# Seven of eight k-tile pairs through Strassen's products, with the first weight sum made by an adding DMA

## The chip, the cores and the metric

The kernel runs on one core of a Trainium2 chip. The metric is the device time of one execution in microseconds (us); the median of several executions counts. The engines are TensorE (PE: matmuls; PEld: its weight loads), VectorE (DVE), ScalarE (ACT), GpSimd (POOL) and SyncE (SP), each with a program order of its own.

## The reference

One encoder layer on 256 positions of width 2048, in float32: a gated feed-forward (FFN) with half weight, a stage of gated mixers, and a second FFN.

```python
def _swiglu(x, w_gate, w_up, w_down):
    return (jax.nn.silu(x @ w_gate) * (x @ w_up)) @ w_down

def _macaron_ffn(x, pre_g, w_gate, w_up, w_down, post_g):
    return x + MACARON_WEIGHT * _rms_norm(_swiglu(_rms_norm(x, pre_g), w_gate, w_up, w_down), post_g)
...
    for l in range(DEPTH):
        h = _macaron_ffn(h, ffn1_pre_g[l], ffn1_w_gate[l], ffn1_w_up[l], ffn1_w_down[l], ffn1_post_g[l])
        h = _gated_mixers(h, mix_pre_g[l], w_in[l], b_gate[l], ...)
        h = _macaron_ffn(h, ffn2_pre_g[l], ffn2_w_gate[l], ffn2_w_up[l], ffn2_w_down[l], ffn2_post_g[l])
```

The hidden width of an FFN is 5632. The change touches the gate and up projections of the two FFNs alone; the mixers (attention, a Fourier branch, projections) stay as they are.

## The kernel before

**Precision.** Every weight piece is split into a high part (a rounded copy that ScalarE makes, `whi`, L104) and a low part (the rest, which VectorE subtracts, `wlo`, L105), and each product is three matmuls (L110 to L112: high by high, low by high, high by low). A tile named `w` holds both parts of a piece in one buffer. A piece is 128 x 1024 (two tiles of 512 columns, "wide" here) or 128 x 512 ("narrow"). So 128 x 1024 of weights cost ScalarE and VectorE one wide operation each, and TensorE 12 matmuls in the plain form.

**Blocks.** An FFN's 5632 hidden columns are 11 blocks of 512. The first two are computed plainly. The other nine of each FFN (18 in all) go through `Line`, a queue of pieces: `feed` adds a piece with what prepares it (its split) and what uses it (its matmuls), and runs the oldest piece's matmuls when eight pieces are waiting (`RING` 6 and `RING_B8` 2). So VectorE and ScalarE work up to eight pieces ahead of TensorE. In these loops the program order on VectorE, ScalarE and TensorE is the order in which the code is written; a piece with `hold` keeps back the preparation of the pieces behind it in the code's order until its use has been written.

One block consists of a **row line** (`row_line`), the down-projection of an earlier block (eight wide pieces, 96 matmuls named `pr`, and eight transposes), and of **eight pairs of k-tiles** of gate and up (`swiglu`, matmuls named `pc`; 16 k-tiles of 128 rows make the depth 2048). At the end of each row column, `out` makes ScalarE copy the sums `pr` into y (`y<-pr`, L696), or into `part`, which GpSimd's adding DMA adds to y (L702).

**Strassen's products.** For a pair of k-tiles the gate and up columns and the two halves of the 256 positions form a 2 x 2 by 2 x 2 block product: plain it takes 8 products (24 matmuls), in Strassen's form 7 (21 matmuls), on prepared sums of the activations (`forms.seven`; the tiles `fh`, `fl`, `frest`) and sums of the weights, which are made for every pair before the split: `minus` (L582, `t<-raw` and `raw<-raw,t`). Here pairs 0, 1, 2, 4, 5, 6 are Strassen's (pieces of 6, 6, 6 and 3 matmuls), pairs 3 and 7 plain (12 and 12). The products p1, p5, p6, p7 gather over the pairs in PSUM banks and are combined once per block, on VectorE, by `add` (L587) between the seventh pair and the end of the plain one: `sums`, `gates`, `ups`. p1, p5, p7 have banks of the pool `ptr`, whose three banks also hold transposes and a few `pr`; p6, g0, g1, u0, u1 have the five of `pmm`.

**Loads.** Weights come by SP's queue (`load`, L85): 512 KB into one of five buffers `raw` (`RAW_BUFS`), and for pairs 0, 2, 4, 6 one load of 1 MB (`raw4`, `RAW_B8`) into a larger buffer of the pool `b8`. A buffer `raw` is free once VectorE has made the low part from it.

Of the kernel before, what the change touches and what calls it, by code (L numbers as in the profile page):

```python
# [45 lines left out]
RAW_B8 = (0, 2, 4, 6)  # L46
# [4 lines left out]
BY_SEVEN = (0, 1, 2, 4, 5, 6)  # L51
# [7 lines left out]
def encoder_layer(  # L59
# [24 lines left out]
    def load(dst, src):  # L84
        nc.sync.dma_start(dst, src)  # L85
# [472 lines left out]
    def swiglu(line, forms, w, hs, behind={}):  # L558
# [22 lines left out]
        def minus(out, a, b):  # L581
            V.tensor_tensor(out=out, in0=a, in1=b, op=ALU.subtract)  # L582

        def add(out, a, b):
            if out not in x:
                x[out] = work(out)
            V.tensor_tensor(out=x[out][:], in0=ps[a][:], in1=x[b][:], op=ALU.add)  # L587
# [5 lines left out]
        def silu(t):  # L593
            g = x["x" + "13"[t]]
            A.activation(g[:], g[:], AF.Silu)

        def times(t):
            g, up = x["x" + "13"[t]], x["x" + "25"[t]]
            V.tensor_tensor(out=up[:], in0=up[:], in1=g[:], op=ALU.mult)
            hs.append(up)  # L600

        def seven(pair, between=None, *then):
            a11, a12, na22, s1, s2, s3, s4 = forms.seven[pair]
            end = pair == BY_SEVEN[-1]
            h = {}

            def first():
                t = chunk.tile([P, WP, NB], F32, tag=("ch_hi", "ch_lo")[BY_SEVEN.index(pair) % 2], name="t13")
                if turn["more"] and pair in RAW_B8:
                    four = big("raw4", F32, [P, 2 * WP, NB])  # L610
                    load(four[:], w[pair // 2].rearrange("p (i k c) -> p i k c", i=2, c=NB)[:, pair % 2])
                    ra, rb = four[:, 0:WP, :], four[:, WP:, :]
                    minus(t[:], four[:, 1:3, :], ra)
                else:
                    ra, rb = raw(pair, 0), raw(pair, 1)
                    minus(t[:, 0, :], ra[:, 1, :], ra[:, 0, :])
# [1 line left out]
                h.update(ra=ra, rb=rb, t=t)
                b = ring(rb[:])
                minus(ra[:, 1, :], rb[:, 0, :], t[:, 0, :])  # L620
                return b

            def second():
                b = ring(h["t"][:])
                minus(h["t"][:, 0, :], h["ra"][:, 1, :], h["rb"][:, 1, :])
                return b

            def two(n, a, m, b, last):
                def use(ws):
                    mul(n, a, ws[0], last)  # L630
                    mul(m, b, ws[1], last)
                return use
# [29 lines left out]
    def row_line(line, ch, w, rb, y, way, ahead):
# [663 lines left out]
def _pairs(g, u):  # L1326
# [57 lines left out]
```

## Time and profile before

| | us |
|---|---|
| time, median of 3 (2003.26 to 2007.38) | 2003.29 |
| profiled execution, its span | 2004.2 |
| TensorE busy | 1984.0 (99%) |
| VectorE busy | 1780.1 (89%) |
| ScalarE busy | 1301.2 (65%) |
| GpSimd busy | 84.5 (4%) |
| one block of the first FFN, from 282.07 to 344.16 | 62.09 |
| its pairs of k-tiles, from 304.73 | 39.43 |

The result lists no own time for the profiled execution beside its span: 2004.2 us is from its first to its last instruction, 0.9 us over the median. A matmul's "busy" is longer than the distance to the next one, since matmuls overlap; the time of a row of matmuls is read from their starts. Two columns in rows of instructions are the start in us from the span's start and the duration; what stands in square brackets is the idle time of the engine ahead of the instruction and what ended it.

### The profile page before, as it was taken

To read this page: it belongs to the slowest core of one execution; us is meant where nothing else is said; L and a number is where in the kernel's file an instruction comes from. 1 tells how busy PE (TensorE), PEld (TensorE's weight loads), DVE (VectorE), ACT (ScalarE), POOL (GpSimd) and SP (SyncE) were. 2 spreads that over 40 slices of the span, in tenths; PEclk is the share of its full clock that TensorE was granted. 3 is DMA by queue.
4 is the path that set the end of the run, shared out by engine and by line. 5 is a ranking of instruction groups with operands and counts; after the bars stand their busy time and mean duration, and the time that the engine had idled before them with its cause. 6 is when DMAs were issued, how large, how long until landed. Compare 5 with 4: busy or idle time off the path is not lost.

```text
span 2004.2 us, 25805 instructions
## 1 busy us (share of the span) xinstructions
PE 1984.0 (99%) x9146; PEld 1644.8 (82%) x9146; DVE 1780.1 (89%) x2352; ACT 1301.2 (65%) x1860; POOL 84.5 (4%) x94
## 2 busy tenths in 40 slices
PE   9999999999999999999999999999999999999998
PEld 7888888888888878888888888878888888888886
DVE  6899999999999878886877885878999999999996
ACT  7566766767667756556666564656677766677666
POOL 0000000000000000100000000000000000000002
PEclk9999999999999999999999999999999999999999
DMA  8657766677668796954555557565577766677673
GB/s 319 211 175 240 225 232 199 200 249 228 226 204 275 250 280 201 261 184 138 195 189 188 192 166 277 194 215 194 169 236 231 231 210 208 213 233 229 208 264 126
DMA packets 117585, 434.20 MB, mean 217 GB/s; under 512 B 12840, under 2 KB 18992, under 8 KB 106064
## 3 DMA queue, kind: packets, MB, share of 16 engines
q1 hardware_dynamic: 103888, 411.65, 59.9%
q0 software_dynamic: 13568, 20.91, 6.0%
q8 instruction: 71, 1.16, 0.2%
q14 instruction: 58, 0.48, 0.1%
HBM read 409.44 MB, written 6.29 MB: 207 GB/s over the span
## 4 chain that ended last, share of the span: by engine, by line
PE 90%; DVE 5%; DMA 3%; ACT 1%; issue 1%; SPq 0%; DVEq 0%; ACTq 0%
PE pc L111 18%; PE pc L112 18%; PE pc L110 18%; PE pr L112 10%; PE pr L111 10%; PE pr L110 10%; DVE wlo L105 2%; PE pt L180 1%; DMA raw<-in_f_gu 1%; DMA raw<-in_w_fo 1%; DVE t L582 0%; PE pe L110 0%; PE pe L112 0%; PE pe L111 0%; PE pt L1072 0%
## 5 line engine op out<-in xcount | busy, mean ns | idle before, releaser
L105 DVE TENSOR_TENSOR wlo<-raw,whi 128x1024 fp32r<-128x1024 f32 (+1 forms) x567 | 681.1, 1219 | 96.9 <-ACT whi L104 95.2
L104 ACT ACTIVATE whi<-raw 128x1024 fp32r<-128x1024 f32 (+1 forms) x567 | 585.8, 1052 | 253.7 <-PE pc L112 109.3
L111 PE MATMUL pc<-wlo,fh 128*128 128x512 f32 x738 | 287.3, 389 | 0.0
L112 PE MATMUL pc<-whi,fl 128*128 128x512 f32 x738 | 287.3, 389 | 0.0
L110 PE MATMUL pc<-whi,fh 128*128 128x512 f32 x738 | 287.1, 389 | 0.0
L110 PE MATMUL pc<-whi,uh 128*128 128x512 f32 x688 | 271.7, 395 | 1.5 <-ACT uh L786 1.5
L111 PE MATMUL pc<-wlo,uh 128*128 128x512 f32 x688 | 269.8, 392 | 1.7 <-DVE wlo L105 1.7
L112 PE MATMUL pc<-whi,ul 128*128 128x512 f32 x688 | 269.6, 392 | 0.0
L104 ACT ACTIVATE whi<-t 128x1024 fp32r<-128x1024 f32 (+1 forms) x198 | 171.6, 867 | 139.4 <-DVE t L582 130.8
L582 DVE TENSOR_TENSOR t<-raw 128x512 f32<-128x512 f32 (+1 forms) x252 | 209.1, 842 | 14.1 <-DMA raw<-in_f_gu 10.3
L110 PE MATMUL pr<-whi,hTh 128*128 128x512 f32 x544 | 213.4, 392 | 0.0
L112 PE MATMUL pr<-whi,hTl 128*128 128x512 f32 x544 | 211.8, 389 | 0.0
L111 PE MATMUL pr<-wlo,hTh 128*128 128x512 f32 x544 | 211.7, 389 | 0.0
L105 DVE TENSOR_TENSOR wlo<-t,whi 128x1024 fp32r<-128x1024 f32 (+1 forms) x198 | 193.6, 978 | 13.4 <-ACT whi L104 13.0
L104 ACT ACTIVATE w<-raw 128x1024 fp32r<-128x1024 f32 x144 | 152.0, 1055 | 40.8 <-DVE raw L582 34.7
L105 DVE TENSOR_TENSOR w<-raw,w 128x1024 fp32r<-128x1024 f32 x144 | 175.6, 1219 | 0.0
L111 PEld LDWEIGHTS pc<-wlo,fh 128*128 128x128 f32 x738 | 138.5, 188 | 29.2 <-DVE wlo L105 0.3
L110 PEld LDWEIGHTS pc<-whi,fh 128*128 128x128 f32 x738 | 138.5, 188 | 28.9
L112 PEld LDWEIGHTS pc<-whi,fl 128*128 128x128 f32 x738 | 138.5, 188 | 28.7
L111 PEld LDWEIGHTS pc<-wlo,uh 128*128 128x128 f32 x688 | 129.8, 189 | 28.5 <-DVE wlo L105 3.6
L110 PEld LDWEIGHTS pc<-whi,uh 128*128 128x128 f32 x688 | 129.7, 188 | 28.5 <-ACT uh L786 2.8
L112 PEld LDWEIGHTS pc<-whi,ul 128*128 128x128 f32 x688 | 129.6, 188 | 27.0
(360 smaller groups left out, 3188.4 us busy)
## 6 DMA issues: line engine op xcount, KB each, us to landing
raw<-in_f_down SPq DMA_DIRECT2D x176, 512.0 KB, 5.0
raw<-in_f_gu SPq DMA_DIRECT2D x144, 512.0 KB, 4.8
raw<-in_f_gu SPq DMA_DIRECT2D x72, 1024.0 KB, 7.0
raw<-in_w_in SPq DMA_DIRECT2D x112, 512.0 KB, 4.5
raw<-in_f_up SPq DMA_DIRECT2D x32, 512.0 KB, 4.5
raw<-in_w_ao SPq DMA_DIRECT2D x32, 512.0 KB, 3.8
raw<-in_w_out SPq DMA_DIRECT2D x32, 512.0 KB, 4.5
raw<-in_f_gate SPq DMA_DIRECT2D x31, 512.0 KB, 5.8
```

The costliest lines, as they stand in the source:

```text
L104: a = A.activation(hi, src, AF.Copy)
L105: v = V.tensor_tensor(out=lo, in0=src, in1=hi.bitcast(F32), op=ALU.subtract)
L110: T.matmul(ps, lh, rh, start=first, stop=False, skip_group_check=onto)
L111: T.matmul(ps, lh, rl, start=False, stop=False, skip_group_check=onto)
L112: return T.matmul(ps, ll, rh, start=False, stop=last, skip_group_check=onto)
L180: T.transpose(pt[:, j, :], src[:, j * P:(j + 1) * P], ident[:])
L582: V.tensor_tensor(out=out, in0=a, in1=b, op=ALU.subtract)
```

## The change

Pair 3 becomes a Strassen pair too; pair 7 alone stays plain. A Strassen pair's weights are combined in another way. The gate columns g0, g1 (512 KB) are loaded into `raw`, the up columns u0, u1 (512 KB) into a tile `ra` in one of six homes that `Sums` hands out (buffers of `b8` and of `chunk`); a DMA on GpSimd's queue adds g0 (256 KB) from memory onto the first half of `ra`. `Sums.get` keeps these loads three pairs ahead (`SUMS_AHEAD`). VectorE then makes one narrow difference `s` (L638) and, once `raw` has been split, one wide difference that overwrites `raw` (L642). The 1 MB loads go. The pieces of a Strassen pair are 6, 6, 3, 6 matmuls. The products are named and combined anew: three combinations instead of four in `sums` (`combine`, L616), and the plain products of u1 are added in the bank of p5 once x4 = p5 - x2 has read it (`onto`), so that the output is x3 - p5. The pool `pmm` then has four names in the block instead of five, and one `pr` moves there from `ptr`. The weights' order in memory for Strassen pairs is the plain one.

```diff
-RAW_B8 = (0, 2, 4, 6)
-BY_SEVEN = (0, 1, 2, 4, 5, 6)
+BY_SEVEN = (0, 1, 2, 3, 4, 5, 6)
+SUMS_AHEAD = 3
...
+    class Sums:
+        def __init__(self, wgu, blocks):
+            self.todo = [(wgu[f], pair) for f in range(blocks) for pair in BY_SEVEN]
+            self.ready, self.n = [], 0
+        def place(self):
+            n = self.n = self.n % 6 + 1
+            if n % 3 == 0:
+                return chunk.tile([P, WP, NB], F32, tag=("ch_hi", "ch_lo")[n // 6], name="ra")
+            if n % 3 == 1:
+                self.two = big("ra2", F32, [P, 2, WP, NB])
+            return self.two[:, n % 3 - 1]
+        def fetch(self):
...
+            ra = self.place()
+            load(ra[:, :, :], src[:, 1])
+            nc.gpsimd.dma_start(ra[:, 0, :], src[:, 0, 0], accum_op=ALU.add)
+            self.ready.append(ra)
+        def get(self):
+            while len(self.ready) <= SUMS_AHEAD and self.todo:
+                self.fetch()
+            return self.ready.pop(0)
...
-                        mul("gu"[i] + str(t), forms.plain[k][t], b[j], k == KD - 1)
+                        n = ("g0", "g1", "u0", "p5")[NT * i + t]
+                        mul(n, forms.plain[k][t], b[j], k == KD - 1, n == "p5")
...
             def first():
-                t = chunk.tile([P, WP, NB], F32, tag=("ch_hi", "ch_lo")[BY_SEVEN.index(pair) % 2], name="t13")
-                if turn["more"] and pair in RAW_B8:
-                    four = big("raw4", F32, [P, 2 * WP, NB])
-                    load(four[:], w[pair // 2].rearrange("p (i k c) -> p i k c", i=2, c=NB)[:, pair % 2])
...
+                h["b"], h["a"], h["s"] = raw(pair, 0), sums_.get(), work("s")
+                V.tensor_tensor(out=h["s"][:], in0=h["a"][:, 0, :], in1=h["a"][:, 1, :], op=ALU.subtract)
+                return ring(h["b"][:])
             def second():
...
+                V.tensor_tensor(out=h["b"][:], in0=h["s"][:].unsqueeze(1).to_broadcast([P, WP, NB]), in1=h["b"][:],
+                                op=ALU.subtract)
+                return ring(h["a"])
...
-            line.feed(first, two("u0", s4, "g0", a12, False))
-            line.feed(second, two("p5", s1, "p7", s3, end), hold=end)
-            line.feed(lambda: ring(h["ra"][:]), two("p1", a11, "p6", s2, end), *then[0:2], hold=end)
-            line.feed(lambda: ring(h["t"][:, 0:1, :]), lambda ws: mul("g1", na22, ws[0]), *then[2:], hold=end)
+            line.feed(first, lambda ws: (mul("p1", a11, ws[0], end), mul("g0", a12, ws[1])))
+            line.feed(second, lambda ws: (mul("p5", s1, ws[0], end), mul("u0", s4, ws[1])), *then[0:1], hold=end)
+            line.feed(lambda: ring(h["s"][:].unsqueeze(1)), lambda ws: mul("p6", s2, ws[0], end), *then[1:3], hold=end)
+            line.feed(lambda: ring(h["b"][:]), lambda ws: (mul("p7", s3, ws[0], end), mul("g1", na22, ws[1])), *then[3:],
+                      hold=end)
...
-        sums = [copy, lambda: add("x2", "p6", "x1"), lambda: add("x3", "p7", "x2"), lambda: add("x2", "p5", "x2"),
-                lambda: add("x5", "p5", "x3")]
+        sums = [copy, lambda: combine("x2", "p6", "x1", ALU.add), lambda: combine("x4", "p5", "x2", ALU.subtract),
+                lambda: combine("x3", "p7", "x2", ALU.add)]
...
-        ups = [lambda: add("x2", "u0", "x2"), lambda: times(0), lambda: add("x5", "u1", "x5"), lambda: times(1)]
+        ups = [lambda: combine("x4", "u0", "x4", ALU.add), lambda: times(0),
+               lambda: combine("x3", "p5", "x3", ALU.subtract), lambda: times(1)]
...
-        rooms = {(0, 0): (ptr, "tr"), (1, 0): (ptr, "tr"), (1, 1): (ptr, "tr")} if not first else {}
+        rooms = {(0, 0): (ptr, "tr"), (1, 0): (ptr, "tr")} if not first else {}
```

VectorE in the pairs of a block before, the end of one pair and the whole of the next, with one plain piece (`raw_2299`) in between (`t13` is the tile `t` of the differences, `raw4` a 1 MB load, `hTl` the low part of the transposed hidden values; where a name ends in a number it is one buffer's):

```order
L105 TENSOR_TENSOR wlo_2241<-raw_2183,whi_2240 128x1024
L105 TENSOR_TENSOR wlo_2259<-t13_2182,whi_2258 128x512
L582 TENSOR_TENSOR t13_2270<-raw4_2271 128x1024
L105 TENSOR_TENSOR w2_2274<-raw4_2271,w2_2274 128x1024
L582 TENSOR_TENSOR raw4_2271<-raw4_2271,t13_2270 128x512
L105 TENSOR_TENSOR wlo_2287<-t13_2270,whi_2286 128x1024
L582 TENSOR_TENSOR t13_2270<-raw4_2271 128x512
L105 TENSOR_TENSOR wlo_2302<-raw_2299,whi_2301 128x1024
L105 TENSOR_TENSOR wlo_2310<-raw4_2271,whi_2309 128x1024
```

and in the changed kernel, one pair at the same place and the first row of the next (`ra2` is the home of the sums):

```order
L638 TENSOR_TENSOR s_2318<-ra2_1901 128x512
L105 TENSOR_TENSOR w2_2320<-raw_2314,w2_2320 128x1024
L642 TENSOR_TENSOR raw_2314<-s_2318,raw_2314 128x1024
L105 TENSOR_TENSOR wlo_2333<-ra2_1901,whi_2332 128x1024
L105 TENSOR_TENSOR wlo_2341<-s_2318,whi_2340 128x512
L105 TENSOR_TENSOR wlo_2353<-raw_2314,whi_2352 128x1024
L638 TENSOR_TENSOR s_2367<-ra_2136 128x512
```

The four wide and three narrow operations of a pair became four wide and two narrow, and `raw` is overwritten in the row behind the one that splits it (`w2`).

ScalarE at the end of the row line before, from the last transposed hidden values (`hTh`) on; the two rows `y<-pr` are the copies of the last row column:

```order
L104 ACTIVATE hTh<-pt 128x4x128 x2
L104 ACTIVATE whi<-raw 128x1024
L696 ACTIVATE y_941<-pr 128x512
L696 ACTIVATE y_942<-pr 128x512
L104 ACTIVATE whi<-t_2722 128x512
L104 ACTIVATE w_2814<-raw_2811 128x1024
```

and now:

```order
L104 ACTIVATE hTh<-pt 128x4x128 x2
L104 ACTIVATE w_2834<-s 128x512
L706 ACTIVATE y_950<-pr 128x512
L706 ACTIVATE y_951<-pr 128x512
L104 ACTIVATE whi<-raw 128x1024 x2
L104 ACTIVATE whi<-ra 128x1024
L104 ACTIVATE w_2891<-s 128x512
```

The copies stand at the same place of the row line; the split behind them was a narrow one (`t`), and is a wide one (`raw`).

VectorE at the end of a block before, from the last splits of the seventh pair on; the rows of L587 and L599 are the combinations:

```order
L105 TENSOR_TENSOR w_2466<-raw_2441,w_2466 128x1024
L105 TENSOR_TENSOR wlo<-t_2440,whi 128x512
L105 TENSOR_TENSOR wlo<-raw,whi 128x1024 x2
L105 TENSOR_TENSOR w_2508<-raw,w_2508 128x1024
L105 TENSOR_TENSOR wlo<-raw,whi 128x1024 x2
L587 TENSOR_TENSOR x_2546<-pc,x_2544 128x512
L587 TENSOR_TENSOR x_2551<-pc,x_2546 128x512
L587 TENSOR_TENSOR x_2546<-pc,x_2546 128x512
L587 TENSOR_TENSOR x_2554<-pc,x_2551 128x512
```

and now (waits in brackets; L616 and L628 are the combinations):

```order
L105 TENSOR_TENSOR wlo<-s,whi 128x512 [waits Activation_49]
L105 TENSOR_TENSOR wlo<-raw,whi 128x1024 [waits Activation_49]
L105 TENSOR_TENSOR w_2539<-raw,w_2539 128x1024 [waits DMAHW6_49,Activation_49]
L105 TENSOR_TENSOR wlo<-raw,whi 128x1024 [waits DMAHW7_49,Activation_49]
L105 TENSOR_TENSOR wlo<-raw,whi 128x1024 [waits DMAHW0_49,Activation_49]
L105 TENSOR_TENSOR wlo<-raw,whi 128x1024 [waits DMAHW1_49,Activation_49]
L105 TENSOR_TENSOR w_2583<-raw,w_2583 128x1024 [waits DMAHW2_49,Activation_49]
L616 TENSOR_TENSOR x_2597<-pc,x_2592 128x512 [waits PE_49,Activation_49]
L616 TENSOR_TENSOR x_2599<-pc,x_2597 128x512 [waits DVE_49]
L616 TENSOR_TENSOR x_2607<-pc,x_2597 128x512 [waits PE_49]
L616 TENSOR_TENSOR x_2592<-pc,x_2592 128x512 [waits PE_49]
```

The five wide splits ahead of the combinations are the same; the second combination is now x4, that which reads p5.

TensorE at the end of the pairs, in the changed kernel, with its waits; `pc_2323` is the bank of p5, `pc_2327` that of u0, `frest` the activations, and `pr` starts the next row line:

```order
L110 MATMUL pc_2327<-whi_2550,frest_1008 128x512
L111 MATMUL pc_2327<-wlo_2551,frest_1008 128x512
L112 MATMUL pc_2327<-whi_2550,frest_1008 128x512
L110 MATMUL pc_2323<-whi_2550,frest_1008 128x512 [waits DVE_49]
L111 MATMUL pc_2323<-wlo_2551,frest_1008 128x512
L112 MATMUL pc_2323<-whi_2550,frest_1008 128x512
L110 MATMUL pc_2323<-whi_2550,frest_1011 128x512
L111 MATMUL pc_2323<-wlo_2551,frest_1011 128x512
L112 MATMUL pc_2323<-whi_2550,frest_1011 128x512
L110 MATMUL pr_2670<-whi_2559,hTh_2256 128x512 [waits Activation_49]
```

Before, the same six matmuls went to a bank of their own (u1) and had no wait for VectorE at that place:

```order
L110 MATMUL pc_2423<-whi_2496,fh_867 128x512
L111 MATMUL pc_2423<-wlo_2497,fh_867 128x512
L112 MATMUL pc_2423<-whi_2496,fl_868 128x512
L110 MATMUL pc_2423<-whi_2496,frest_996 128x512
L111 MATMUL pc_2423<-wlo_2497,frest_996 128x512
L112 MATMUL pc_2423<-whi_2496,frest_996 128x512
L110 MATMUL pr_2617<-w2_2508,hTh_2212 128x512 [waits Activation_49]
L111 MATMUL pr_2617<-w2_2508,hTh_2212 128x512 [waits DVE_49]
```

So the wait in front of `pc_2323` is new; the row line's first matmul, with its wait for ScalarE, stands behind it.

More of the change, by code (lines that the diff above doesn't have):

```diff
@@ L556, in end, with swiglu, mul @@
                 self.next()
-    def swiglu(line, forms, w, hs, behind={}):
+    class Sums:
[10 more added lines that the diff above has]
+        def fetch(self):
+            if not self.todo:
+                return
+            w, pair = self.todo.pop(0)
+            src = w[pair // 2].rearrange("p (q i k c) -> p q i k c", q=2, i=2, c=NB)[:, pair % 2]
+            ra = self.place()
[6 more added lines that the diff above has]
+            return self.ready.pop(0)
+    def swiglu(line, forms, w, sums_, hs, behind={}):
         ps, begun, x = {}, set(), {}
-        def mul(n, a, b, last=False):
+        def mul(n, a, b, last=False, onto=False):
             if n not in ps:
-                ps[n] = ptr.tile([P, NB], F32, tag="tr", name="pc") if n in ("p5", "p7", "p1") else                     pmm.tile([P, NB], F32, tag="mm", name="pc")
-            mm3(ps[n][:], *a, *b, n not in begun, last)
+                ps[n] = ptr.tile([P, NB], F32, tag="tr", name="pc") if n in ("p5", "p7", "p1") else \
+                    pmm.tile([P, NB], F32, tag="mm", name="pc")
+            mm3(ps[n][:], *a, *b, n not in begun, last, onto)
             begun.add(n)
@@ L593, in silu, with seven @@
         def silu(t):
-            g = x["x" + "13"[t]]
+            g = x["x" + "12"[t]]
             A.activation(g[:], g[:], AF.Silu)
         def times(t):
-            g, up = x["x" + "13"[t]], x["x" + "25"[t]]
+            g, up = x["x" + "12"[t]], x["x" + "43"[t]]
             V.tensor_tensor(out=up[:], in0=up[:], in1=g[:], op=ALU.mult)
             hs.append(up)
-        def seven(pair, between=None, *then):
+        def seven(pair, *then):
             a11, a12, na22, s1, s2, s3, s4 = forms.seven[pair]
@@ L618, in first @@
[L618 to L621, printed above, removed]
-            def second():
[L624 to L632, printed above, removed]
@@ L645, in swiglu @@
+        gates = [lambda: combine("x1", "g0", "x1", ALU.add), lambda: combine("x2", "g1", "x3", ALU.add),
+                 lambda: silu(0), lambda: silu(1)]
+        ups = [lambda: combine("x4", "u0", "x4", ALU.add), lambda: times(0),
+               lambda: combine("x3", "p5", "x3", ALU.subtract), lambda: times(1)]
         for kg in range(KD // CK):
@@ L647, in swiglu @@
             if kg == KD // CK - 1:
-                seven(a, None, *sums)
+                seven(a, *sums)
                 if a in behind:
@@ L652, in swiglu @@
                 plain(b, 1, *ups)
-            elif b in BY_SEVEN:
+            else:
                 seven(a)
@@ L740, in ffn @@
         line = Line()
+        sums_ = Sums(wgu, nblk - PLAIN)
         end = []
@@ L757, in ffn @@
                     turn["more"] = True
-                    swiglu(line, forms, wgu[f - PLAIN], hs, {
+                    swiglu(line, forms, wgu[f - PLAIN], sums_, hs, {
                         5: lambda: end.append(tail(y)), 6: lambda: end.extend(end.pop()())} if f == nblk - 1 else {})
@@ L1331, in _pairs @@
     out = np.stack([g[:, :, 0], g[:, :, 1], u[:, :, 0], u[:, :, 1]], 3)
-    for q in BY_SEVEN:
-        out[:, q] = np.stack([g[:, q, 0], u[:, q, 0], u[:, q, 1], g[:, q, 1]], 2)
     out = out.reshape(-1, KD // CK, 2, P, 4 * NB).transpose(0, 1, 3, 2, 4)
```

18 lines of the change are left out of this document (2 added, 16 removed).

## The prediction

> **What bounds the kernel now.** I read the busy table first, then TensorE's waits, then two FFN blocks as stretches of time, then single instructions.
>
> ```profile
> PE 1984.0 (99%) x9146; PEld 1644.8 (82%) x9146; DVE 1780.1 (89%) x2352; ACT 1301.2 (65%) x1860; POOL 84.5 (4%) x94
> PE pt L180 <- DVE y L418: 2.5, 1, 2.5
> PE pc L111 <- DVE wlo L105: 1.7, 4, 0.7
> 282.07:344.16 62.09, 62.09 (x279) 51.50 (x278) 60.46 (x70) 42.38 (x53) 3.49 (x4) 1.00 0.69 219
> 1513.76:1575.99 62.23, 62.23 (x280) 51.51 (x278) 61.01 (x70) 42.07 (x53) 3.52 (x4) 1.00 0.70 222
> 304.73:344.16 39.43, 39.43 (x175) 32.66 (x174) 38.82 (x44) 23.18 (x26) 0.00 (x0) 1.00 0.53 173
> 342.81 0.39 PE L110 MATMUL pc<-whi,fh 128*128 128x512 f32 x1
> ...
> 343.94 0.39 PE L112 MATMUL pc<-whi,frest 128*128 128x512 f32 x1
> 344.17 0.39 PE L110 MATMUL pr<-w,hTh 128*128 128x512 f32 x1
> ```
>
> TensorE is busy 99% of the span, and its longest waits on the other engines are 2.5 and 1.7 us in all. The two block rows (columns: length, then busy time of PE, PEld, DVE, ACT, POOL, granted clock, DMA share, GB/s) show one block of each FFN: TensorE is busy in all of it, but VectorE in 60.46 of 62.09 us. So TensorE sets the block, and VectorE has 1.6 us left over, with its work spread unevenly. In the matmul rows 342.81 to 344.17 six starts take 1.36 us, 0.2267 us each. The third window, from 304.73 on, is the eight pairs of k-tiles alone; what precedes it is the row line of the block before (down-projection). I work the change out in the block that starts at 282.07 and take it 18 times.
>
> **TensorE loses work.** One pair per block goes from 24 matmuls to 21: 3 x 0.2267 = 0.68 us a block, 18 x 3 = 54 matmuls, -12.2 us in all. This lies on the bounding engine and would be a full gain if nothing else gave way.
>
> **VectorE's cost of a Strassen pair.** These are its instructions at the start of the pairs, then ScalarE's beside them.
>
> ```profile
> 305.04 1.22 DVE L105 TENSOR_TENSOR wlo<-raw,whi 128x1024 fp32r<-128x1024 f32 x1
> 306.17 0.69 DVE L105 TENSOR_TENSOR wlo<-t,whi 128x512 fp32r<-128x512 f32 x1
> 306.77 1.22 DVE L582 TENSOR_TENSOR t<-raw 128x1024 f32<-128x1024 f32 x1
> 307.90 1.22 DVE L105 TENSOR_TENSOR w<-raw,w 128x1024 fp32r<-128x1024 f32 x1
> 309.04 0.69 DVE L582 TENSOR_TENSOR raw<-raw,t 128x512 f32<-128x512 f32 x1
> 309.64 1.22 DVE L105 TENSOR_TENSOR wlo<-t,whi 128x1024 fp32r<-128x1024 f32 x1
> 310.90 0.69 DVE L582 TENSOR_TENSOR t<-raw 128x512 f32<-128x512 f32 x1
> ```
> ```profile
> 303.63 0.60 ACT L696 ACTIVATE y<-pr 128x512 f32<-128x512 f32 x1 [0.29 <-PE pr L112]
> 304.99 0.60 ACT L696 ACTIVATE y<-pr 128x512 f32<-128x512 f32 x1 [0.76 <-PE pr L112]
> 305.48 0.63 ACT L104 ACTIVATE whi<-t 128x512 fp32r<-128x512 f32 x1
> 306.00 1.05 ACT L104 ACTIVATE w<-raw 128x1024 fp32r<-128x1024 f32 x1
> ```
>
> From start to start a wide operation takes 1.13 to 1.14 us (306.77 to 307.90 to 309.04), a narrow one 0.60; an operation that needs the result of the one just before it starts 0.12 later (309.64 to 310.90 is 1.26). A Strassen pair issues now three wide and two narrow splits, and its sums become one narrow difference s, which reads the two halves that the adding DMA and a load left, and one wide difference, which overwrites `raw` right behind the split of `raw` and so waits for it. That is 4 x 1.135 + 2 x 0.605 + 0.12 = 5.87 us, against 21 x 0.2267 = 4.76 us of TensorE. Before, such a pair had four wide and three narrow operations (three wide splits and a narrow one, a wide difference and two narrow ones), 4 x 1.135 + 3 x 0.605 + 0.12 = 6.5 us. It is cheaper, but the plain pair in the middle, in which VectorE needed 2 x 1.135 = 2.27 us against TensorE's 24 x 0.2267 = 5.44, is gone. Per block that is 34 wide and 34 narrow before, 38 wide and 25 narrow after: 4 x 1.135 - 9 x 0.605 = -0.9 us, so the sum of VectorE's work falls by 0.9 us, about as TensorE's does.
>
> **What starts the chain.** VectorE cannot run ahead as it likes. ScalarE's copy of the last row column, `y<-pr` at 304.99, waits 0.76 us for TensorE to finish the row line; behind it in ScalarE's order stands the split of the next piece (305.48), and VectorE's low part at 306.17 follows it. So in each block the pieces behind that copy start when the row line ends. Before, the first of them was narrow; now it is the wide last piece of the second pair. By the rows above ScalarE does 305.48 + 1.06 = 306.54, VectorE starts at 306.60 and is through at 307.73. Five Strassen pairs follow: 307.73 + 5 x 5.87 = 337.08. This is the block's end on VectorE as it is now:
>
> ```profile
> 334.94 0.68 DVE L105 TENSOR_TENSOR wlo<-t,whi 128x512 fp32r<-128x512 f32 x1
> 335.62 2.36 DVE L105 TENSOR_TENSOR wlo<-raw,whi 128x1024 fp32r<-128x1024 f32 x2
> 337.90 1.22 DVE L105 TENSOR_TENSOR w<-raw,w 128x1024 fp32r<-128x1024 f32 x1
> 339.03 2.36 DVE L105 TENSOR_TENSOR wlo<-raw,whi 128x1024 fp32r<-128x1024 f32 x2
> 341.30 4.53 DVE L587 TENSOR_TENSOR x<-pc,x 128x512 f32<-128x512 f32 x7
> ```
>
> Five wide splits (two of the plain pair, three of the next row line) stand ahead of the combinations at 341.30. They do so again: 337.08 + 5 x 1.135 = 342.76 is when x2 starts, and x4 = p5 - x2, which needs it, ends about 0.73 + 0.69 later, at 344.2.
>
> **The new wait.** Now u1's six plain products are added in p5's own PSUM bank, so TensorE may write it only when x4 has read p5. Behind that wait stand the block's last six matmuls and then the next row line. TensorE would be there after 7 x 21 + 18 = 165 matmuls: 304.73 + 165 x 0.2267 = 342.14. It waits 2.1 us. Before, u1 had a bank of its own and nothing waited there, so the same lateness cost nothing.
>
> **The load in front of it.** All Strassen pairs now take `raw` from the five buffers, the pieces of plain pair and row line too. The third row piece's buffer is the one of the seventh pair, free only with that pair's last split, about 337.1. The load and two splits stand between this and x2. What loads take:
>
> ```profile
> DMA to landing us min/median/max: 3.1/4.8/9.8
> ...
> L85 SPq DMA_DIRECT2D raw<-in_f_down x1: 327/327/327, 461.1 to 461.1; - x1
> ...
> DMA to landing us min/median/max: 3.9/3.9/3.9
> ```
>
> The first row is all raw loads; the other two a load with no other in flight from its queue. At 3.1 us nothing is delayed, at 4.8 x4 comes 1.5 us later than by VectorE alone. I take 4.0, near the lone load: landing 341.2, ScalarE's wide split to 342.3, VectorE's to 343.5, x4 through at 344.9; TensorE waits 2.85 us. (The Trainium skill's page "DMA: Bandwidth & Descriptors", section "Anatomy of one DMA — SWDGE (gpsimd) path", fits 2.0 us plus bytes at 436 GB/s; for 512 KB that is an estimated 3.2 us, by which this load would cost next to nothing and the sum would be 13 us less. The lone load's 3.9 speaks against it.)
>
> **The clock after the wait.** The trace shows what follows an idle TensorE elsewhere, in consecutive stretches of 3.41 us:
>
> ```profile
> 779.75:783.17 3.42, 2.25 (x11) 1.51 (x9) 2.11 (x6) 1.24 (x5) 0.00 (x0) 1.00 0.94 208
> 783.17:786.58 3.41, 3.41 (x18) 2.94 (x19) 3.41 (x6) 3.20 (x3) 0.73 (x1) 1.00 0.55 198
> ...
> 892.40:895.81 3.41, 1.90 (x15) 1.51 (x13) 2.18 (x5) 1.50 (x3) 0.00 (x0) 1.00 0.79 257
> 895.81:899.23 3.42, 3.42 (x17) 3.13 (x16) 3.35 (x5) 1.08 (x3) 0.00 (x0) 0.50 0.47 156
> ```
>
> With 1.2 us idle (the first) the next stretch kept its clock; with 1.5 idle (the third) it ran at 0.50. A wait of 2.85 us leaves at least 1.4 idle in one stretch wherever it falls, so nearly every block would lose up to half of 3.41 us, less where part of the slow stretch is spent waiting; I take 1.4 us. The ends are 0 and 1.7. (The Trainium skill's page "TensorE: Matmul & The Clock Gate", section "HAM oscillation — how this bites in real kernels", speaks of idle gaps over about 3.4 us. By that no wait here would halve the clock and the sum would lack this term, 25 us; the row at 895.81 says otherwise, and I go by the row.)
>
> **The adding DMA and the rest.** Seven 256 KB adding DMAs a block come on GpSimd's queue, 126 in all. The nearest rows are those of y's adding DMAs and of the queues:
>
> ```profile
> L702 POOL DMA_DIRECT2D y<-part x32: 847/941/1219, 168.2 to 608.9; - x32
> ...
> DMA to landing us min/median/max: 6.0/7.5/11.1
> ...
> q1 hardware_dynamic: 103888, 411.65, 59.9%
> q0 software_dynamic: 13568, 20.91, 6.0%
> ...
> 98.21 1.29 DVE L484 TENSOR_TENSOR un<-uh,ul 128x512 f32<-128x512 f32 x2
> 107.52 1.22 DVE L582 TENSOR_TENSOR t<-raw 128x1024 f32<-128x1024 f32 x1
> ```
>
> They are issued three pairs ahead, at least 3 x 5.87 = 17 us before they are read; 4.8 (load) + 7.5 fit, so they cost nothing there; GpSimd's seven issues, 7 x 0.94 = 6.6 us a block, lie beside its 3.5 busy. In the first block of each FFN this cover is missing: the homes become free about 98.9 (row 98.21), the load and the sum land 12.3 later at 111.2, and the first pair's sums ran at 107.52; with what slack there is I take 2.7 each, 5.4 us (ends 0 and 2 x 3.7). The queue rows give 0.06 x 16 x 2004 / 20.91 = 92 engine-us per MB, so 1.84 MB a block make 10.6 us on each of 16 engines: the block's DMA share goes from 0.69 to about 0.86. If that queue delays the loads, they are what is late next. The 1 MB loads of four pairs become two of 512 KB each, the same bytes in four more issues on SP's queue; their cost is in the late load above.
>
> **The sum.** -12.2 + 18 x 2.85 + 18 x 1.4 + 5.4 = -12.2 + 51.3 + 25.2 + 5.4 = +69.7 us. The profiled execution's span is 2004.2, the median 2003.3; the difference of 0.9 is nothing beside this. Forecast: 2073 us.
>
> **Rivals.**
> *Faster.* The wait at p5 is not there because the chain is shorter than I add it up: x4 needs to end 2.1 us earlier, which is 0.4 us on each of five pairs. For it speaks that VectorE has 0.9 us less work per block; against it the 1.135 and 0.605 of the rows, which hardly vary. Then TensorE bounds as before: 2003.3 - 12.2 = 1991, or 1996 with the first blocks' 5.4; it decides where x4 is through by 342.1. If x4 is 0.4 us late on average and the clock stays, the block is -0.3 and the time about 1998 + the 5.4 of the first blocks: no difference.
> *The wait without its sequels.* By VectorE's chain alone, 2003.3 - 12.2 + 18 x 2.1 + 5.4 = 2034; with the late load but a full clock, 2048; with the clock but an early load, 2059. (The skill's rule on idle gaps, above, would lead to the second of these.)
> *Late transfers.* At a share of 0.86 loads take their median, 4.8, or more instead of 4.0: 18 x 0.8 = 14 more, 2088; at 5.5, 2100. The share was 0.69 with a 4.8 median, so this is real, but the row-line load falls in the second part of a block, where the share was 0.53.
> *That the change does not do what it says* is excluded for TensorE: its program has 54 matmuls fewer.
>
> **Chances.** Forecast (wait, late load, slow clock) 0.42; wait without one or both sequels 0.28; late transfers 0.13; faster 0.13; no difference 0.04. Within 0.2% (4 us) a measurement of this kernel cannot tell a change from none. The range from 2020 to 2100 takes in the second and third and most of the fourth and leaves out the last two, some 2 in 10. Slower 0.42 + 0.28 + 0.13 = 0.83, same 0.04, faster 0.13.
>
> **What would show it.** Right: TensorE's matmul count 54 lower; a wait of TensorE for VectorE's x4 (L616) of 2 to 3 us, 18 times; blocks of about 65.9 us; a granted clock of 0.50 in the 3.41 us behind each wait; ScalarE waiting for a down-projection load ahead of the wait. Wrong: blocks of 61.4 us with TensorE at 100%; a Strassen pair on VectorE well under 5.8 us; ScalarE's copy of the row no longer holding the pieces back; or VectorE waiting for the adding DMA inside the blocks, by which the wait would lie at the pairs and not at p5.

## The result, and the profile after

The changed kernel takes 2064.99 us (median of 4, 2057.76 to 2067.22) against 2004.84 before; the ratio is 1.029, with a 95% interval of 1.0278 to 1.0303. Forecast were 2073 us and a range of 2020 to 2100. The profiled execution has a span of 2064.8 us, 60.6 over that of before.

The busy table, TensorE's waits for other engines (engine, line, waited for: us in all, times, longest), and two blocks, from one row line's first matmul to the next, of the changed kernel:

```profile
PE 1995.0 (97%) x9092; PEld 1639.4 (79%) x9092; DVE 1767.7 (86%) x2276; ACT 1323.4 (64%) x1906; POOL 193.7 (9%) x220
...
PE pc L110 <- DVE x L616: 34.5, 18, 3.1
PE pc L111 <- DVE wlo L105: 8.3, 20, 0.8
PE pc L110 <- DVE hTl L105: 5.8, 2, 2.9
PE pr L110 <- ACT yf L706: 2.4, 1, 2.4
...
229.70:294.06 64.36, 62.16 (x276) 50.78 (x275) 59.42 (x64) 43.37 (x56) 8.78 (x10) 1.00 0.78 229
360.28:425.87 65.59, 62.42 (x277) 51.01 (x276) 58.65 (x63) 42.63 (x54) 8.72 (x10) 0.99 0.77 224
```

TensorE has its 54 matmuls fewer and VectorE is busy 12 us less, yet the kernel is slower: L616 is x4, for which TensorE now waits 18 times, once per block. A block takes 64.36 or 65.59 us where it took 62.09. The waits are idle time alone. With the slow restart behind it a wait costs some 0.3 us more (at the wait of 2.11 us that ends at 490.36, 0.16 us up to that matmul's start and 0.10 up to the next), which "lost" below includes: the distance between two starts less 0.2267.

VectorE over one Strassen pair of the block between those two (from 294.06 to 360.28, 66.22 us) and at its end, then ScalarE, then TensorE and the granted clock behind the wait (columns as in the prediction):

```profile
320.28 1.22 DVE L105 TENSOR_TENSOR wlo<-raw,whi 128x1024 fp32r<-128x1024 f32 x1
321.53 1.23 DVE L642 TENSOR_TENSOR raw<-s,raw 128x1024 f32<-128x1024 f32 x1
322.67 1.22 DVE L105 TENSOR_TENSOR wlo<-ra,whi 128x1024 fp32r<-128x1024 f32 x1
323.81 0.69 DVE L105 TENSOR_TENSOR w<-s,w 128x512 fp32r<-128x512 f32 x1
324.41 1.22 DVE L105 TENSOR_TENSOR wlo<-raw,whi 128x1024 fp32r<-128x1024 f32 x1
325.55 0.68 DVE L638 TENSOR_TENSOR s<-ra 128x512 f32<-128x512 f32 x1
326.15 1.22 DVE L105 TENSOR_TENSOR wlo<-raw,whi 128x1024 fp32r<-128x1024 f32 x1
...
352.43 1.22 DVE L105 TENSOR_TENSOR wlo<-raw,whi 128x1024 fp32r<-128x1024 f32 x1
354.94 1.22 DVE L105 TENSOR_TENSOR wlo<-raw,whi 128x1024 fp32r<-128x1024 f32 x1 [1.29 <-ACT whi L104]
356.09 3.80 DVE L616 TENSOR_TENSOR x<-pc,x 128x512 f32<-128x512 f32 x6
```
```profile
353.85 1.06 ACT L104 ACTIVATE whi<-raw 128x1024 fp32r<-128x1024 f32 x1 [2.65 <-DMA raw<-in_f_down]
```
```profile
354.69 0.39 PE L112 MATMUL pc<-whi,frest 128*128 128x512 f32 x1
357.55 0.80 PE L110 MATMUL pc<-whi,frest 128*128 128x512 f32 x1 [2.47 <-DVE x L616]
358.14 0.63 PE L111 MATMUL pc<-wlo,frest 128*128 128x512 f32 x1
358.57 0.63 PE L112 MATMUL pc<-whi,frest 128*128 128x512 f32 x1
...
357.01:360.42 3.41, 2.87 (x7) 2.30 (x8) 3.31 (x6) 1.70 (x3) 0.00 (x0) 0.50 0.87 330
```

A pair takes 326.15 - 320.28 = 5.87 us, as was added up. The chain ends as forecast too: ScalarE waits 2.65 us for a down-projection load, VectorE's last split ahead of the combinations waits 1.29 us for ScalarE, and x4, the second of the six at 356.09, releases TensorE at 357.55. The matmuls behind it start 0.43 us apart instead of 0.23: the clock is halved, 0.50 from 357.01 to 360.42. That happens behind six of the 18 waits for x4.

Where the 60.6 us are, from the starts of the row lines (each FFN's first block apart):

| | before | after | difference |
|---|---|---|---|
| 16 blocks (62.09 to 62.27 each before, 64.11 to 66.22 after) | 994.6 | 1040.4 | +45.8, 2.86 each |
| first block of FFN 1 and of FFN 2 | 62.1 + 62.9 | 69.4 + 72.3 | +16.7 |
| all else | | | -1.9 |

In the 16 blocks TensorE loses 2.9 us each to waits (1.6 to 3.2 at x4, 0.6 at the low part of the seventh pair's last piece, the rest their restarts) and 0.5 to half-clocked matmuls, and saves 0.68.

### The profile page after: what moved, and what is told of

It is laid out like the page before. It is cut to its first block, busy times and chain, and to the rows that moved or that the text cites. A ratio compares the mean times of both kernels' runs of the same rounds, so it can differ in the third digit from the quotient of the medians.

```text
span 2064.8 us, 26338 instructions
## 1 busy us (share of the span) xinstructions
PE 1995.0 (97%) x9092; PEld 1639.4 (79%) x9092; DVE 1767.7 (86%) x2276; ACT 1323.4 (64%) x1906; POOL 193.7 (9%) x220
## 3 DMA queue, kind: packets, MB, share of 16 engines
q0 software_dynamic: 31712, 53.95, 15.3%
## 4 chain that ended last, share of the span: by engine, by line
PE 58%; DVE 26%; DMA 8%; issue 5%; ACT 2%; POOL 0%; SPq 0%; DVEq 0%; ACTq 0%; POOLq 0%
DVE wlo L105 13%; PE pr L110 10%; PE pr L111 10%; PE pr L112 10%; PE pc L110 8%; PE pc L111 8%; PE pc L112 8%; DVE raw L642 5%; DMA raw<-in_f_down 3%; DVE w L105 3%; DVE s L638 2%; DMA ra<-in_f_gu 2%; ACT whi L104 1%; PE pt L180 1%; DVE x L616 1%
## 5 line engine op out<-in xcount | busy, mean ns | idle before, releaser
L105 DVE TENSOR_TENSOR wlo<-raw,whi 128x1024 fp32r<-128x1024 f32 (+1 forms) x603 | 726.1, 1218 | 166.9 <-ACT whi L104 165.6
L104 ACT ACTIVATE whi<-raw 128x1024 fp32r<-128x1024 f32 (+1 forms) x603 | 621.5, 1054 | 380.1 <-PE pc L112 134.0
L111 PE MATMUL pc<-wlo,fh 128*128 128x512 f32 x675 | 265.6, 394 | 6.6 <-DVE wlo L105 6.6
L110 PE MATMUL pc<-whi,fh 128*128 128x512 f32 x675 | 263.8, 391 | 5.8 <-DVE hTl L105 5.8
L112 PE MATMUL pc<-whi,fl 128*128 128x512 f32 x675 | 263.7, 391 | 0.0
L580 POOL DMA_DIRECT2D ra<-in_f_gu x126 | 111.3, 883 | 1207.1 <-ACT fh L104 545.0
L642 DVE TENSOR_TENSOR raw<-s,raw 128x1024 f32<-128x1024 f32 x126 | 154.4, 1225 | 4.3
L105 DVE TENSOR_TENSOR wlo<-ra,whi 128x1024 fp32r<-128x1024 f32 x126 | 153.7, 1219 | 5.1 <-ACT whi L104 4.7
L104 ACT ACTIVATE whi<-ra 128x1024 fp32r<-128x1024 f32 x126 | 132.7, 1053 | 21.1 <-issue 11.3
L104 ACT ACTIVATE w<-raw 128x1024 fp32r<-128x1024 f32 x108 | 113.4, 1050 | 36.8 <-DMA raw<-in_f_gu 19.0
```

Of the source, the lines that this page charges most:

```text
L104: a = A.activation(hi, src, AF.Copy)
L105: v = V.tensor_tensor(out=lo, in0=src, in1=hi.bitcast(F32), op=ALU.subtract)
L110: T.matmul(ps, lh, rh, start=first, stop=False, skip_group_check=onto)
L111: T.matmul(ps, lh, rl, start=False, stop=False, skip_group_check=onto)
L112: return T.matmul(ps, ll, rh, start=False, stop=last, skip_group_check=onto)
L580: nc.gpsimd.dma_start(ra[:, 0, :], src[:, 0, 0], accum_op=ALU.add)
```

## The experiments

Eleven kernels, each against the kernel before on the same chip (whose median there was 2005.5 to 2007.1). All edits are to the changed kernel, but for one.

| kernel | us | ratio to before (95%) |
|---|---|---|
| own_bank_pair3_plain | 2017.0 | 1.0052 (1.0035 to 1.0068) |
| old_sums_seven | 2067.2 | 1.0306 (1.0290 to 1.0321) |
| own_bank | 2053.8 | 1.0228 (1.0212 to 1.0245) |
| third_load_reused | 2040.8 | 1.0172 (1.0156 to 1.0187) |
| no_adding_dma | 2049.6 | 1.0210 (1.0193 to 1.0227) |
| late_copy | 2056.0 | 1.0245 (1.0227 to 1.0262) |
| s_on_gpsimd | 2092.4 | 1.0434 (1.0415 to 1.0453) |
| first_sum | 2049.4 | 1.0228 (1.0201 to 1.0254) |
| early_x4 | 2020.6 | 1.0068 (1.0054 to 1.0082) |
| early_late_first | 2005.7 | 0.9998 (0.9989 to 1.0006) |
| later_copy_too | 2003.0 | 0.9985 (0.9975 to 0.9994) |

**One pair fewer: own_bank_pair3_plain.**

```diff
-BY_SEVEN = (0, 1, 2, 3, 4, 5, 6)
+BY_SEVEN = (0, 1, 2, 4, 5, 6)
-                        n = ("g0", "g1", "u0", "p5")[NT * i + t]
+                        n = ("g0", "g1", "u0", "u1")[NT * i + t]
+            elif b not in BY_SEVEN:
+                seven(a)
+                plain(b, 0)
+                plain(b, 1)
```

(With u1's bank go a tile x5 = p5 - x3, to which u1 is added, and the third room of the row line in `ptr`, as before.)

> As own_bank, and pair 3 plain again, so that the new sums (loads ahead, adding DMA, narrow and wide difference) are used for six pairs as before. Theory A: no wait of TensorE inside blocks, 62.1 us each, the first blocks' loss of about 10 us alone: 2010 to 2016. Theory C (the adding DMAs' traffic delays the weights, whatever the order on VectorE): six sevenths of the traffic remain, so blocks stay over 63 us and the time over 2025.

A block of this kernel:

```profile
225.11:287.20 62.09, 62.09 (x279) 51.50 (x278) 56.50 (x60) 41.79 (x54) 8.69 (x10) 1.00 0.83 249
```

Measured 2017.0, 1 us over the forecast of theory A. The block is back at 62.09 us with TensorE busy throughout, at a DMA share of 0.83; VectorE has 4 us less to do than before the change (56.50 against 60.26 to 60.46). So neither the new sums nor the traffic of the adding DMAs, six a block here instead of seven, cost anything in a block. The 10 us that are left lie in the first blocks, 67.40 and 68.32 us against 62.12 and 62.90 before.

**The seventh pair in the old form: old_sums_seven**, in the kernel before:

```diff
-BY_SEVEN = (0, 1, 2, 4, 5, 6)
+BY_SEVEN = (0, 1, 2, 3, 4, 5, 6)
```

> The kernel before with nothing changed but that pair 3 goes through Strassen's products too, with the old sums on VectorE (no adding DMA, u1 in a bank of its own). Theory A2 (the seventh pair takes away the relief on which VectorE lived; each Strassen pair costs it 6.5 us against 4.76 of TensorE): VectorE has 4.2 us more work per block and becomes the bound, blocks of 64 to 66.5 us with TensorE waiting for low parts inside the pairs: 2004.8 + 18 x (2 to 4.5) = 2040 to 2086, at least as slow as the changed kernel's blocks. Theory B2 (the new sums, their loads and the adding DMA are what costs): 1992 to 2010.

```profile
227.13:292.72 65.59, 63.66 (x276) 50.30 (x275) 64.33 (x75) 43.85 (x55) 3.48 (x4) 1.00 0.65 207
...
PE pc L111 <- DVE wlo L105: 17.5, 49, 0.8
PE pc L111 <- DVE w L105: 15.8, 45, 0.8
```

2067.2 us, without any adding DMA and with u1 in its own bank. VectorE works 64.33 of 65.59 us and is the bound; TensorE waits for it in short pieces, five or so a block, inside the pairs. So it is the seventh pair that turns the block: it takes away the plain pair in the middle, on which VectorE caught up. The new sums pay for all of that work (58.65 and 59.42 us of VectorE in the two blocks shown of the changed kernel, 60.26 and 60.46 in two blocks before), but not for the order in which it falls due.

**u1's own bank, nothing else: own_bank** (the second hunk of the first diff).

> u1's plain products get a PSUM bank of their own again; nothing else is changed but one more combination on VectorE. Theory A (the bank shared by p5 and u1 turns VectorE's lateness at the block's end into a wait of TensorE, which costs 1.4 to 3.2 us a block and halves the clock behind some): TensorE's waits for L616 fall from 34.5 us to under 3, the small wait for the low part of the seventh pair's last piece (0.6 to 0.7 us lost a block) stays, no half clock in the blocks, blocks of 62.1 us, and the first block of each FFN stays slow: 2004.8 - 12.2 + 18 x 0.7 + 10 = 2015 us. Theory B (VectorE itself bounds the block, the bank only shows it): the wait moves to the next row line, blocks stay over 64 us, about 2055 to 2065.

```profile
PE pr L110 <- ACT pr L696: 25.3, 16, 2.5
PE pc L111 <- DVE wlo L105: 10.0, 21, 1.0
```

2053.8: nearer to theory B, and not what the prediction would have had. The wait at x4 is gone, but another stands in its place, in the next row line, 12 us on: ScalarE's `pr<-y`. This is ScalarE in between:

```profile
295.50 1.23 ACT L624 ACTIVATE x<-x 128x512 f32<-128x512 f32 x2 [4.05 <-DVE x L616]
296.63 2.94 ACT L104 ACTIVATE whi<-raw 128x1024 fp32r<-128x1024 f32 x3
299.48 1.04 ACT L104 ACTIVATE w<-raw 128x1024 fp32r<-128x1024 f32 x1
300.43 1.04 ACT L104 ACTIVATE whi<-raw 128x1024 fp32r<-128x1024 f32 x1
303.63 1.06 ACT L104 ACTIVATE whi<-raw 128x1024 fp32r<-128x1024 f32 x1 [2.16 <-DMA raw<-in_f_gu]
304.60 1.10 ACT L696 ACTIVATE pr<-y 128x512 f32<-128x512 f32 x2
```

It waits 4.05 us for VectorE's combinations (silu, L624) with six splits and `pr<-y` queued behind. The last of the six waits another 2.16 us for a load; that load was issued at 300.01, when VectorE's first split behind its combinations (298.77) had freed the buffer, so it too is late by VectorE's order. The shared bank cost 0.6 us a block (the 16 blocks take 1031.6 us against 1040.4); the other 2.3 stay with a bank of its own, and go back to VectorE's lateness, whichever instruction shows it. Own_bank_pair3_plain differs from this kernel by pair 3 alone and takes 2017.0.

**The order at the block's end: early_x4.** The pieces of the sixth and seventh Strassen pair hold back the splits of the next row line, until x4 (`...` inside a line stands for what is left out of it):

```diff
+pre = pair == BY_SEVEN[-2]
-line.feed(first, lambda ws: (mul("p1", ...), mul("g0", ...)))
+line.feed(first, lambda ws: (mul("p1", ...), mul("g0", ...)), hold=end)
-... mul("p6", s2, ws[0], end), *then[1:3], hold=end)
+... mul("p6", s2, ws[0], end), *then[1:3], hold=pre)
-... mul("g1", na22, ws[1])), *then[3:], hold=end)
+... mul("g1", na22, ws[1])), *then[3:], hold=end or pre)
```

> The changed kernel with another order of the same instructions at the block's end: the splits of the next row line's first pieces are held back until x2 and x4 have been made, and go behind them on VectorE and ScalarE. Theory A (of VectorE's lateness only what stands ahead of x4 counts): three wide splits, 3.4 us, and the late load leave the way to x4, which is then 1 us in time; waits for L616 under 3 us in all, the 0.7 us at the low part of the seventh pair stay, no half clocks: blocks of 62.1, 2004.8 - 12.2 + 18 x 0.7 + 10 = 2015. Theory B (own_bank already pointed to it: VectorE and ScalarE are late as a whole, and any order only moves the wait): TensorE waits in the next row line for splits or for pr<-y, blocks of 63.5 us or more, 2045 or more.

```profile
288.16:350.38 62.22, 61.85 (x276) 50.87 (x275) 59.46 (x63) 43.01 (x56) 11.34 (x13) 1.00 0.93 273
```

2020.6: theory A, some 6 us over its number (2.7 of them between the FFNs' blocks). No wait for x4 is left, and none has come elsewhere in the blocks: TensorE still loses 0.6 us at the low part of the seventh pair's last piece, in blocks of 62.2 to 62.4. So theory B holds only while the order stands: VectorE's work fits the block (59.46 of 62.22 us); three row-line splits and a late load stood ahead of the one instruction for which TensorE waited.

**The load: third_load_reused.** The third row piece is split from the second's buffer again, its load left out:

```diff
+            if first or (cb, i) != (1, 0):
+                kept["raw"] = raw_piece(w[rb, cb], i)
+            return ring(kept["raw"][:])
```

> The changed kernel with the load of the row line's third piece left out in every block: its split reads the second piece's buffer once more, so no load stands between the seventh pair's last split and x4. By the prediction's step on the late load, x4 comes when VectorE alone allows it: TensorE loses about 2.1 us at x4 and the low part before it together, instead of 2.5 to 4.1: 18 x 0.9 = 16 us less, and with fewer halved clocks 5 to 10 less again: 2038 to 2046. If the load did not matter: 2060 to 2066.

```profile
PE pc L110 <- DVE x L616: 19.5, 18, 1.1
```

2040.8, inside the forecast. All 16 blocks now take 63.56 to 63.65 us, lose about 2.1 to waits, and none has a halved clock. So the 2.1 us are VectorE's chain alone, and everything by which blocks differed (up to 66.22) came from this load and the clock behind it: 1.4 us a block. (The edit also takes 512 KB of traffic and one turn of the five buffers `raw` out of each block; no run separates these from the load itself.)

**Without the adding DMAs: no_adding_dma** (the line at L580 left out).

> The changed kernel without its 126 adding DMAs: the first weight sum lacks g0, all else is the same. Theory A: VectorE's chain is the same, so TensorE still waits for x4 in every block, but the late load in front of it comes 0.5 to 1 us earlier and the first blocks lose about 4 instead of 10 us: 2040 to 2055. Theory C (traffic): the waits vanish, 1995 to 2010.

2049.6. The first blocks take 64.24 and 64.31 us, 13 less than with the adding DMA; the other 16 average 64.86 against 65.03. So this DMA costs 0.2 us in a block, where 0.5 to 1 had been expected, and 13 us at the two starts; TensorE still waits 18 times for x4, 32.7 us in all, so this traffic is not the cause. **first_sum** takes that away more finely: the first pair of each FFN gets its sum from VectorE.

```diff
+            if self.fetched:
+                nc.gpsimd.dma_start(ra[:, 0, :], src[:, 0, 0], accum_op=ALU.add)
...
+                if alone:
+                    V.tensor_tensor(out=h["a"][:, 0, :], in0=h["a"][:, 0, :], in1=h["b"][:, 0, :], op=ALU.add)
```

> The changed kernel, but the very first pair of each FFN gets its weight sum from VectorE (one narrow addition of 0.6 us) instead of the adding DMA. Theory: the first block of each FFN (69.4 and 72.3 us) loses 3.5 and 6.5 us because VectorE waits for load and adding DMA one behind the other (7.2 and 6.1 us), so this takes 6 to 7 us from each: 2050 to 2055. If the loss is the first load alone: 2060 or more.

2049.4; the first blocks fall from 69.40 and 72.32 to 65.03 and 67.41, 9.3 us together where 12 to 14 had been expected. The 16 other blocks, whose sums the edit does not touch, take 1034.8 us against 1040.4, for which the record gives no cause; without these 5.6 us the time would have been about 2055. In the changed kernel VectorE stood there like this:

```profile
106.62 1.23 DVE L105 TENSOR_TENSOR wlo<-raw,whi 128x1024 fp32r<-128x1024 f32 x1 [0.68 <-ACT whi L104]
113.91 0.69 DVE L638 TENSOR_TENSOR s<-ra 128x512 f32<-128x512 f32 x1 [6.07 <-DMA ra<-in_f_gu]
```

**What starts VectorE's chain: late_copy.** The last row column's copies are handed to the next pair's first piece:

```diff
+                if outs and cb == D // NB - 1 and way != "add":
+                    line.late, outs = outs, []
...
+            late, line.late = line.late, []
-            line.feed(first, lambda ws: (mul("p1", ...), mul("g0", ...)))
+            line.feed(first, lambda ws: (mul("p1", ...), mul("g0", ...)), *late)
```

> The changed kernel with ScalarE's copies of the last row column (y<-pr) put one piece later in the program, behind the split that they held back. The prediction's step on what starts VectorE's chain: that split then waits only for its ring buffer, which is free when the row line ends, so the chain starts about 0.65 us earlier (two copies of 0.52 and the start). TensorE loses 0.65 us less per block and some halved clocks fall away: 2065 - 12 - 5 = 2048. If the copies did not hold the chain: 2060 to 2068.

```profile
PE pc L110 <- DVE x L616: 32.0, 18, 2.9
PE pc L111 <- DVE wlo L105: 3.1, 5, 0.8
```

2056.0, between the two: the wait at the seventh pair's low part is gone (lost 0.6), the one at x4 is as it was, since the load ahead of x4 decides there. The copies did hold the chain, and it was worth 0.4 to 0.5 us in an undisturbed block (63.7 against 64.2).

**Moving VectorE's work away: s_on_gpsimd** (`nc.gpsimd.tensor_tensor` at L638).

> The changed kernel with the narrow difference s made by GpSimd instead of VectorE; nothing else moves. Theory A2: a Strassen pair costs VectorE 5.27 instead of 5.87 us, over the five pairs behind the row line 3.0 us, so x4 is in time (TensorE lost 2.1 to 3.2 us there and at the low part before it); blocks of 61.4 to 62 us, first blocks as slow as before: 2004.8 - 12.2 + 10 = 2003, up to 2015 if loads still come late. Theory D (GpSimd is slow, sits behind its adding DMAs, or disturbs VectorE): s comes late or VectorE's operations grow longer; 2060 or more.

2092.4: theory D. GpSimd, with its group in this kernel, and VectorE's low part of `ra` in the changed kernel and in this one (times, busy us, mean ns):

```profile
L638 POOL TENSOR_TENSOR s<-ra 128x512 f32<-128x512 f32 x126 | 234.2, 1871 | 194.5 <-DMA ra<-in_f_gu 174.1 <-DMA y<-part 5.1 <-DMA yf<-part 4.4
```
```profile
L105 DVE TENSOR_TENSOR wlo<-ra,whi 128x1024 fp32r<-128x1024 f32 x126 | 153.7, 1219 | 5.1 <-ACT whi L104 4.7
```
```profile
L105 DVE TENSOR_TENSOR wlo<-ra,whi 128x1024 fp32r<-128x1024 f32 x126 | 207.2, 1644 | 7.4 <-ACT whi L104 7.4
```

The difference takes GpSimd 1.87 us against VectorE's 0.68, and VectorE's own instructions grow: its busy time is 1816.9 us, 49 more than in the changed kernel, though 126 instructions of 0.68 us have left it. So the experiment says nothing on theory A2.

**Together: early_late_first** is early_x4, late_copy and first_sum in one.

> early_x4, late_copy and first_sum together. Theory A: early_x4 takes the wait at x4, late_copy the one at the low part of the seventh pair, first_sum 6 us or more in each first block; what is left is TensorE's own time, blocks of 61.5 us, and some 4 us in the first blocks: 2004.8 - 12.2 + 4 = 1997, faster than before by 0.4%. Theory B: as under early_x4, 2030 or more.

2005.7, no difference from before: theory A's mechanism, not its number. Blocks take 61.92 us, with 0.33 still lost at the low part, so they give back only 0.2 to 0.3 each, 2.9 in all 18. Between the FFNs' blocks, where no line is edited, 2.1 us are lost again, 1.9 of them in one wait of TensorE (`pt<-o`, 2.28 us where it was 0.40); no run shows why. **later_copy_too** moves the copies one more piece on:

> early_late_first with ScalarE's copies of the last row column one more piece later. In early_late_first TensorE still lost 0.33 us a block at the low part of the seventh pair's last piece, since VectorE's second split behind the row line waited 0.17 us for ScalarE, which was at those copies. Theory A (every tenth of VectorE's chain behind the row line counts until that wait is gone): blocks fall from 61.92 to 61.6 to 61.75 us, 18 x 0.2 to 0.3 = 4 to 5 us, 2001 against 2005.5 before. Rival E (the copies then hold PSUM or GpSimd's adding DMA of y too long): blocks as before or longer, 2005 or more.

```profile
282.67:344.40 61.73, 61.73 (x276) 50.87 (x275) 59.42 (x63) 42.91 (x56) 11.31 (x13) 1.00 0.93 275
```

2003.0 against 2005.7 before on the same chip, a ratio of 0.9985: its interval leaves out 1, but 0.15% is less than the 0.2% that the prediction named as the least that can be told from none. All but one of the 16 blocks behind the first ones are at 61.73 to 61.75, with TensorE busy throughout; together they take 988.1 us against 994.6, 6.5 of the 10.9 that their saved matmuls are worth. Of these 6.5, 1.6 go again in the two first blocks (63.3 us each) and 3.5 between the FFNs' blocks, 1.7 of them in the same `pt<-o`.

## Why the prediction was right, and where it was off

- *TensorE loses work, 0.68 us a block:* right; later_copy_too shows 0.4 of it once the waits are gone.
- *A Strassen pair costs VectorE 5.87 us:* measured 5.87.
- *What starts the chain:* right in time (in the block quoted, the split behind the copies starts 24.5 us after the row line's first matmul, by the prediction 306.60 - 282.07 = 24.5). Late_copy shows that the copies account for 0.4 to 0.5 us of it.
- *The new wait:* the place was right, the reason only in part. The prediction put it down to the shared bank: before, with a bank for u1, "the same lateness cost nothing". Own_bank has that bank again and still loses 2.3 of the 2.86 us a block, 12 us into the next row line. What makes the lateness cost is the order: the prediction counted the three splits and the load ahead of x4 into the chain, but not that they could as well stand behind it (early_x4).
- *Its size, and the load in front of it:* the sum of 2.85 us a block was met (2.9), in part by luck, since the 2.9 contain some 0.5 us of restarts that the prediction did not have; the idle time is 2.3. The shape was another too. The prediction had VectorE late at x4 alone; it was already late at the seventh pair's last piece, and the loss came as 0.6 there and 1.6 to 3.2 at x4. Third_load_reused confirms 2.1 of it, restarts included, as VectorE's chain. The load ahead of x4 took 3.60 to 5.22 us from issue to landing in the 16 blocks, 4.1 on average, where 4.0 had been taken; so the rival of late transfers (4.8 or more throughout) did not come.
- *The clock after the wait, 1.4 us a block:* mis-sized; it was 0.5, behind six of 18 waits and not behind nearly all. The rule taken from one row, that 1.5 us idle in a stretch halve the clock of the next, does not hold here. These are two pairs of consecutive stretches of 3.41 us of the changed kernel, laid out from the clock change at 554.98; the first pair is around a wait of 2.11 us that fell across both, the second around one of 1.82 that fell into one:

```profile
486.73:490.14 3.41, 1.52 (x7) 0.91 (x5) 2.47 (x4) 1.47 (x2) 0.00 (x0) 1.00 0.95 348
490.14:493.55 3.41, 3.19 (x14) 2.64 (x15) 3.31 (x7) 2.02 (x3) 0.00 (x0) 1.00 1.02 406
...
551.57:554.98 3.41, 1.59 (x7) 1.01 (x6) 2.83 (x4) 0.99 (x2) 0.00 (x0) 1.00 0.98 330
554.98:558.40 3.42, 3.42 (x9) 2.65 (x9) 3.32 (x6) 2.50 (x4) 0.00 (x0) 0.50 0.83 315
```

  With 1.89 us idle in its stretch the clock stayed, with 1.82 it fell to 0.50: near that value the idle time alone does not decide. Of the 18 waits 13 left 1.4 us or more idle in one stretch; behind seven of these (1.48 to 1.89 idle) the clock stayed. (The Trainium skill's "TensorE: Matmul & The Clock Gate", section "HAM oscillation — how this bites in real kernels", names idle gaps over about 3.4 us; the trace halves the clock behind shorter ones, here 1.82, and the trace decides.)
- *The first blocks, 5.4 us:* mis-sized the other way; 11 more than the other blocks' excess (16.7 - 2 x 2.86). The load and the adding DMA landed at 113.9 where 111.2 was added up, and in the second FFN the loss was larger still. No_adding_dma puts 13 us there.
- *The adding DMA inside a block, nothing:* right (0.2 us), at queue costs as forecast (15.3% for 53.95 MB are 94 engine-us per MB, against 92).
- *The rivals:* the faster one needed x4 2.1 us earlier; early_x4 and later_copy_too got there by order alone. That they end near before and not at 1991 was not foreseen. In later_copy_too the 16 blocks give back 6.5 us and 5.1 are lost elsewhere; why is not shown.

The two errors of size, 18 x 0.9 = 16 us too much for the clock and some 6 too little for the starts, make most of the 8 us between 2073 and 2065; that they partly cancel is luck. What stays open: why blocks with the same order have the load late in some and not in others, and what decides over the clock between 1.8 and 1.9 us idle.

## What to carry to other kernels

Taking work off the bounding engine pays only if the helper that feeds it keeps its slack where it is needed: compare, stretch by stretch between two points at which the helper must wait, what it has to do with what the bound engine does, and not the totals of the block, which fell here for both. If a new wait appears on the bounding engine, look first at what merely stands ahead of the awaited instruction in the helper's order: three splits and a load put behind it were worth 44 us here, a bank of its own 11. A transfer that a pipeline hides is still paid in full at the pipeline's start.

## What the runs showed of the hardware that was not expected

GpSimd's difference of two 128x512 float32 halves took 1.87 us, and VectorE's instructions beside it grew, single ones from 1.22 to 2.3 us:

```profile
318.68 1.87 POOL L638 TENSOR_TENSOR s<-ra 128x512 f32<-128x512 f32 x1 [1.09 <-DMA y<-part]
319.32 2.31 DVE L105 TENSOR_TENSOR wlo<-ra,whi 128x1024 fp32r<-128x1024 f32 x1
```

GpSimd's difference ends at 320.55, VectorE's split 1.08 us later, at 321.63. It is not alone: all 89 of VectorE's 128x1024 splits and differences that took over 1.3 us in this run end 1.08 or 1.09 us after the end of one of GpSimd's differences, and in the changed kernel none took that long. So each seems to have waited until the difference was done and to have run then.

The Trainium skill's "SBUF — State Buffer", section "SBUF: two separate sides", has an exclusive lock on a port pair that GpSimd and a VectorE instruction with two SBUF inputs share, by which one of them waits for the whole of the other. The rows agree in this: VectorE's instruction ends a fixed time behind GpSimd's, whenever it started.
